# Mixer's output projection, first half: two-by-two blocks with seven products for eight

## The chip, the core and the metric

The kernel runs on one core of one Trainium2 chip. The time is that of one execution on the device, in microseconds (us). A core has engines that work side by side, each through its own queue in order: TensorE (PE, matrix products; PEld is its loading of weights), VectorE (DVE), ScalarE (ACT), GpSimd (POOL), and SyncE (SP), which issues DMA transfers; GpSimd issues some too. Matrix products are collected in PSUM banks, which ACT and DVE read; operands lie in SBUF.

## The reference: what is computed

One decoder layer for a prompt of 512 tokens and 64 sample tokens (576 columns in all), width 1024. The mixer runs 16 SSM heads and 4 mLSTM heads side by side, gates them, and projects both back to 1024:

```python
y_ssd = (y_ssd + d_skip[:, None] * xs).reshape(bsz, length, SSM_INNER) * jax.nn.silu(z)
y_ssd = _rms(y_ssd.reshape(bsz, length, SSM_GROUPS, SSM_INNER // SSM_GROUPS)).reshape(bsz, length, SSM_INNER) * g_ssm_out
...
h_ml = _rms(h_ml).reshape(bsz, length, ML_INNER) * g_mlstm_out * jax.nn.sigmoid(og)
mix = jnp.concatenate([y_ssd.astype(x.dtype), h_ml.astype(x.dtype)], axis=-1) @ w_out
x = x + _rms(mix) * g_post_mix
```

Cross-attention over a memory and a SwiGLU feed-forward layer follow. The first half of the output projection is `y_ssd` times rows 0 to 1023 of `w_out`, the second half `h_ml` times the other rows.

## The kernel before

**Products.** Activations lie transposed: 8 tiles of 128 channels, 576 columns of tokens. Every operand is split into a high part, rounded to the type that PE takes at full rate (`fp32r`), and a low part, the rest; ACT casts the high part, DVE (or GpSimd) subtracts to get the low one. A product is then three matmuls: high by high, high by low, low by high (L215, L216, L218 in `gemm`). Weights come tile by tile over SP's queue into `raw` (2 buffers), and become `whi` and `wlo` (3 buffers each) in `split_w`.

**Ahead of the change.** The last eight of the input projections (`in_tile(29 + j)`, output `ps_in`) make the output gate, each in two halves of 256 and 320 columns, 24 matmuls a half. `og_evac` takes each half: DVE multiplies it by the row factor into one of two `tmp` buffers (L1133), ACT takes the tanh (L1134), DVE multiplies it onto the mLSTM output in `qk` (L1136), and for the second half GpSimd copies the sample columns to `ogs` (L1138). `ps_in` has three PSUM banks. Between these halves the order places the last of the mLSTM heads: `ps_s`, `dm` (L966, L973), then for each of four chunks `ps_n` (L983, L985), its copy to `num` (L986), `ps_c` (L988) and the state's update (L993); then the head's norm (`head_norm`: ACT's sums of squares L938, small DVE steps L941 to L954, one GpSimd step L950), the scaling of `num` (L1000) and its transposition on PE (`ps_ht`, L1004). `gn_apply` normalises the SSM output in two groups of four tiles (`xs`, L1122) and splits it into `mixs_h` and `mixs_l`.

**The half that changes.** `out1(j)` makes one tile of 128 outputs from 8 tiles of `mixs`, in two halves of columns (256 and 320): 8 x 8 x 3 x 2 = 384 matmuls into `ps_o`, each half copied by ACT to `f_mix` (L1154). Beside it ACT and DVE make `mixm_h` and `mixm_l`, the operands of the second half, from `qk` (L1160, L1161), and `presplit` fetches weight tiles of later stages over GpSimd's queue (`prel`, L1251), splits them on ACT and DVE (L1244, L1245) and stores the low part for later (L1246). The second half, `out2`, adds its products to `f_mix` on DVE (L1288).

**What sets the order.** The program is written stage by stage; a scheduler that knows the tiles and their places in memory orders each engine's queue at build time. `tc.issue_after` holds a step back behind another one. Where a tile takes a place in memory that another one held, it waits for the last user of that place.

Of the kernel before, what the change touches and what calls it, by code (L numbers as in the profile page):

```python
# [11 lines left out]
F32 = mybir.dt.float32  # L12
# [7 lines left out]
P = 128  # L20
T = 576
# [94 lines left out]
def build(nc, tc, ctx, I, O):  # L116
# [324 lines left out]
    ghalf = ml.tile([P, KT], F32, name="ghalf")  # L441
    V.tensor_scalar(ghalf, PAR("g_ml"), 0.5, None, op0=ALU.mult)
# [668 lines left out]
    mixs_l = SL(2, "mixs_l", F32R)  # L1111
    gn_rc = {}
# [4 lines left out]
    def gn_apply(g):  # L1117
# [3 lines left out]
        for j in range(4 * g, 4 * g + 4):  # L1121
            V.scalar_tensor_tensor(y[:, j, :], y[:, j, :], PAR("g_ssm", j), rb, op0=ALU.mult, op1=ALU.mult)  # L1122
            split(mixs_h[:, j, :], mixs_l[:, j, :], y[:, j, :])
# [4 lines left out]
    ogs = zp.tile([P, KT, TS], F32, name="ogs")  # L1128
# [17 lines left out]

    f = SL(5, "f_mix")
    evs = []

    def out1(j):  # L1150

        with tc.issue_after(ht.ins) if j == 0 else ExitStack():
            gemm2([(*split_w(I["wout"][j, 0], cut=1024), KT)], act(mixs_h), act(mixs_l),
                  lambda t0, n, ps: evs.append(A.copy(f[:, j, t0:t0 + n], ps)), "ps_o1")  # L1154

    out1(0)
    for j in range(8):
        hm = qk[:, 4 * (j % 2) + j // 2, 0:TP]
        with tc.issue_after((evs[0] if j > 2 else htc).ins):
            A.activation(mixm_h[:, j, 0:TP], hm, AF.Copy, scale=ghalf[:, j:j + 1])  # L1160
        V.scalar_tensor_tensor(mixm_l[:, j, 0:TP], hm, ghalf[:, j:j + 1], mixm_h[:, j, 0:TP].bitcast(F32),  # L1161
                               op0=ALU.mult, op1=ALU.subtract)
    o4 = ogs.rearrange("p (h d) t -> p h d t", d=2)
    for d in range(2):
        V.scalar_tensor_tensor(o4[:, :, d], o4[:, :, d], 1.0, qk[:, 4 * d:4 * d + 4, TP:T], op0=ALU.add, op1=ALU.mult)
    V.tensor_tensor(ogs, ogs, ghalf.unsqueeze(2).to_broadcast([P, KT, TS]), op=ALU.mult)
    split(mixm_h[:, :, TP:T], mixm_l[:, :, TP:T], ogs)
    stv.close()


# [62 lines left out]
    PRE = [("xo", 0), ("xo", 1), ("g", 0), ("u", 0), ("g", 1), ("u", 1), ("g", 2), ("u", 2)]  # L1233
    pre = dr.tile([P, len(PRE), 1024], F32, name="pre")

    ahead = []

    def presplit(n, left=1):

        while len(ahead) > left:  # L1240
            n_, t_ = ahead.pop(0)
# [20 lines left out]
    for j in range(8):  # L1262
        if j:
            out1(j)
# [1212 lines left out]
```

## Time and profile before

| what | value |
|---|---|
| three runs | 1074.66, 1076.41, 1076.59 us (median 1076.41) |
| the profiled execution | 1074.69 us, its span 1072.9 us |
| granted TensorE clock | 0.999 |
| first half of the output projection | 384.0 to 433.8 us of the span |
| second half | 433.8 to 484.4 us |
| last gate halves, last mLSTM head | 342 to 384 us |

The times of the table's last rows are read from the first and last `ps_o` matmuls. The profile gives each engine's busy time, the chain of work that ended last, groups of instructions (count, busy time, mean of one), a timeline, and busy times by stretch of the span. A matmul's own duration (about 0.3 us) is longer than the distance between two starts, since matmuls are pipelined.

### The profile page before, as it was taken

The page shows a single profiled execution, that of the slowest core. Times are in us where ns is not written, and L with a number is a line of the kernel's source. Part 1 is how long each engine was busy: PE and PEld are TensorE (multiplying, and loading weights), DVE is VectorE, ACT ScalarE, POOL GpSimd, SP SyncE. Part 2 cuts the span into 40 slices and gives each one's busy share as a digit, 9 for nine tenths or more (in the row PEclk, how much of TensorE's full clock was granted, in tenths as well). Part 3 has the DMA queues.
Part 4 walks back from the last instruction along what each step waited for, and adds up shares of the span by engine and source line. Part 5 has one row for each costly group of instructions (what it writes and reads, how often), then busy time and mean ns, then how long its engine had stood idle before and what let it go on. Part 6 is the DMA issues. An engine that isn't in the chain of part 4 may idle for free.

```text
span 1072.9 us, 20686 instructions
## 1 busy us (share of the span) xinstructions
PE 1063.1 (99%) x8096; PEld 1011.0 (94%) x8096; DVE 757.7 (71%) x1523; ACT 608.9 (57%) x1102; POOL 231.0 (22%) x305
## 2 busy tenths in 40 slices
PE   9999999999999999999999999999999999999997
PEld 8999887778999999999999989999999999999997
DVE  6798775658878774758755556766467887787556
ACT  7778523345654555655555445645566566656654
POOL 0454543313213111000154201100011111111000
PEclk9999999999999999999999999999999999999999
DMA  6776544425655349642468775743476687578532
GB/s 209 176 162 132 158 134 172 147 89 168 196 150 152 106 143 330 235 170 98 158 213 288 265 256 176 254 124 98 133 179 137 160 188 178 114 191 188 144 119 89
DMA packets 58965, 181.74 MB, mean 169 GB/s; under 512 B 6604, under 2 KB 12108, under 8 KB 58356
## 3 DMA queue, kind: packets, MB, share of 16 engines
q1 hardware_dynamic: 42884, 138.22, 38.7%
q0 software_dynamic: 15408, 41.43, 19.7%
q8 instruction: 63, 1.03, 0.4%
q10 hardware_dynamic: 576, 0.79, 0.2%
q14 instruction: 34, 0.28, 0.1%
HBM read 159.75 MB, written 20.65 MB: 168 GB/s over the span
## 4 chain that ended last, share of the span: by engine, by line
PE 98%; DVE 0%; DMA 0%; POOL 0%; issue 0%; ACT 0%; SPq 0%; DVEq 0%
PE ps_in L215 7%; PE ps_in L218 7%; PE ps_in L216 7%; PE ps_v L882 5%; PE ps_g L1946 3%; PE ps_u L1946 3%; PE ps_g L1945 3%; PE ps_o L218 3%; PE ps_o L216 3%; PE ps_u L1947 3%; PE ps_g L1947 3%; PE ps_o L215 3%; PE ps_u L1945 3%; PE ps_dn L1945 2%; PE ps_dn L1947 2%; PE ps_dn L1946 2%
## 5 line engine op out<-in xcount | busy, mean ns | idle before, releaser
L215 PE MATMUL ps_in<-uh,whi 128*128 128x320 f32 (+1 forms) x544 | 162.6, 299 | 0.0
L218 PE MATMUL ps_in<-uh,wlo 128*128 128x320 f32 (+1 forms) x544 | 161.6, 298 | 0.0
L216 PE MATMUL ps_in<-ul,whi 128*128 128x320 f32 (+1 forms) x544 | 161.1, 296 | 0.0
L191 ACT CAST whi<-raw 128x1024 fp32r<-128x1024 f32 (+1 forms) x104 | 105.4, 1015 | 93.3 <-PE ps_in L216 21.5
L198 DVE TENSOR_TENSOR wlo<-raw,whi 128x1024 fp32r<-128x1024 f32 (+2 forms) x97 | 95.3, 983 | 63.7 <-ACT whi L191 63.0
L215 PEld LDWEIGHTS ps_in<-uh,whi 128*128 128x128 f32 x544 | 102.3, 188 | 1.9 <-issue 0.8
L218 PEld LDWEIGHTS ps_in<-uh,wlo 128*128 128x128 f32 x544 | 102.2, 188 | 1.9 <-issue 1.3
L216 PEld LDWEIGHTS ps_in<-ul,whi 128*128 128x128 f32 x544 | 102.4, 188 | 0.5
L196 POOL DMA_DIRECT2D wlo<-win x31 | 27.2, 877 | 80.2 <-ACT wlo L195 69.9
L1945 PE MATMUL ps_g<-b,whi 128*128 128x288 f32 x144 | 42.4, 295 | 0.0
L1946 PE MATMUL ps_g<-b,whi 128*128 128x288 f32 x144 | 42.3, 294 | 0.0
L1946 PE MATMUL ps_u<-b,whi 128*128 128x288 f32 x144 | 42.2, 294 | 0.0
L1945 PE MATMUL ps_u<-b,whi 128*128 128x288 f32 x144 | 42.2, 294 | 0.0
L1905 DVE TENSOR_TENSOR wlo<-sw,whi 128x1024 fp32r<-128x1024 f32 (+1 forms) x26 | 29.6, 1139 | 16.8 <-ACT whi L1904 16.8
L1918 ACT CAST whi<-rawx 128x1024 fp32r<-128x1024 f32 (+1 forms) x26 | 25.6, 986 | 26.2 <-PE ps_dn L1946 13.3
L1895 ACT CAST whi<-raw 128x1024 fp32r<-128x1024 f32 (+1 forms) x26 | 25.6, 985 | 22.8 <-PE ps_g L1946 11.8
L215 PE MATMUL ps_xo<-qh,whi 128*128 128x288 f32 x128 | 38.2, 301 | 0.0
L216 PE MATMUL ps_xo<-ql,whi 128*128 128x288 f32 x128 | 37.8, 297 | 0.0
L218 PE MATMUL ps_o<-mixm_h,wlo 128*128 128x256 f32 (+1 forms) x128 | 37.5, 293 | 0.0
L216 PE MATMUL ps_o<-mixm_l,whi 128*128 128x256 f32 (+1 forms) x128 | 37.5, 293 | 0.0
L218 PE MATMUL ps_xq<-u2h,wlo 128*128 128x320 f32 (+1 forms) x128 | 37.5, 294 | 0.0
L218 PE MATMUL ps_o<-mixs_h,wlo 128*128 128x320 f32 (+1 forms) x128 | 37.4, 293 | 0.0
(788 smaller groups left out, 3855.6 us busy)
## 6 DMA issues: line engine op xcount, KB each, us to landing
raw<-win SPq DMA_DIRECT2D x35, 512.0 KB, 4.4
raw<-wout SPq DMA_DIRECT2D x17, 512.0 KB, 4.2
raw<-wxq SPq DMA_DIRECT2D x13, 512.0 KB, 4.7
raw<-wgate SPq DMA_DIRECT2D x13, 512.0 KB, 3.3
raw<-wup SPq DMA_DIRECT2D x13, 512.0 KB, 4.7
wlo<-win POOLq DMA_DIRECT2D x24, 256.0 KB, 5.6
kva<-vc SPq DMA_DIRECT2D x11, 512.0 KB, 5.9
raw<-wv SPq DMA_DIRECT2D x10, 512.0 KB, 4.0
```

Of the source, the lines that this page charges most:

```text
L191: casts.append(A.copy(hi[:, :n], raw[:, :n]))
L196: accs.append(G.dma_start(lo[:, a:b], src[:, a:b], accum_op=ALU.add))
L198: e.tensor_tensor(lo[:, a:b], raw[:, a:b], hi[:, a:b].bitcast(F32), op=ALU.subtract)
L215: mm(ps, wh, ah, start=i == 0, stop=False)
L216: products.append(mm(ps, wh, al, start=False, stop=False))
L218: m = mm(ps, tiles[order[c]][1], xh(order[c], t0, n), start=False, stop=c == len(tiles) - 1)
L882: mm(ps, a, b, skip_group_check=True, **kw)
L1895: s.c1 = A.copy(s.h1[:, s.all], s.r1[:, s.all])
L1905: V.tensor_tensor(s.l2[:, s.all], sw[:, s.all], s.h2[:, s.all].bitcast(F32), op=ALU.subtract)
L1945: mm(ps, wh, b[0][k], start=start and k == 0, stop=False, skip_group_check=True)
L1946: mm(ps, wh, b[1][k], start=False, stop=False, skip_group_check=True)
L1947: m = mm(ps, wl, b[0][k], start=False, stop=k == nk - 1, skip_group_check=True)
```

## The change

The eight output tiles are taken in four pairs. A pair's weights are a two-by-two block matrix (two output tiles by the two halves of the contraction, tiles 0 to 3 and 4 to 7), and the activations are one too (the two halves of the contraction by columns 0 to 287 and 288 to 575). The four blocks of the result are put together from seven products of sums of blocks instead of eight products of blocks. A product is 4 tiles x 3 matmuls of 288 columns; a pair is 84, all four 336.

The sums of activations are made once, in place in the gated SSM output (`xs`; `y` in the code) by GpSimd: four, each 128x4x288, and each is split into `tmh` and `tml` by ACT and DVE. The sums of weights are made for each pair: four GpSimd operations of 128x512, into `swm`, `rawm` and `raw`. `h4` and `ls`, a high and a low part, take columns of `mixs_h` and `mixs_l` that are no longer used. A pair runs as `early` (products 1, 2), then the previous pair's `late` (products 6, 7), then `mid` (3, 4, 5). Some products accumulate onto a bank after ACT has copied it out; `put` copies a block the first time and adds the second time on DVE.

Around it: `ogs` moves to the new pool `mixsums`, the `mixm` parts go behind the casts of pairs 0 and 1, `presplit`'s subtraction goes from DVE to GpSimd and most of its turns to the second half, and the loads of the memory (`memT`) with them.

```diff
@@ gn_apply(g)
-            split(mixs_h[:, j, :], mixs_l[:, j, :], y[:, j, :])
+            c = slice(0, T if g else 288)
+            split(mixs_h[:, j, c], mixs_l[:, j, c], y[:, j, c])
+        for m, o, a, b in ([(2, M12, M22, M12), (1, M22, M22, M11), (3, M21, M21, M22)] if g else [(0, M11, M12, M11)]):
+            G.tensor_tensor(o, a, b, op=ALU.subtract)
+            split(tmh[m], tml[m], o)
...
-    ogs = zp.tile([P, KT, TS], F32, name="ogs")
+    ogs = wo.tile([P, KT, TS], F32, name="ogs")
...
+    def mixm_parts(js, p_):
+        for j in js:
+            hm = qk[:, 4 * (j % 2) + j // 2, 0:TP]
+            with tc.issue_after(p_.cast.ins):
+                A.activation(mixm_h[:, j, 0:TP], hm, AF.Copy, scale=ghalf[:, j:j + 1])
...
-    def out1(j):
-
-        with tc.issue_after(ht.ins) if j == 0 else ExitStack():
-            gemm2([(*split_w(I["wout"][j, 0], cut=1024), KT)], act(mixs_h), act(mixs_l),
-                  lambda t0, n, ps: evs.append(A.copy(f[:, j, t0:t0 + n], ps)), "ps_o1")
...
+    class Mixed:
...
+            s.r1 = wp.tile([P, 1024], F32, name="raw", tag="raw", bufs=2)
+            s.r2 = wv.tile([P, 1024], F32, name="rawm", tag="rawm", bufs=2)
...
+            G.tensor_tensor(sm[:, HB], s.r2[:, HA], s.r2[:, HB], op=ALU.add)
+            split(h1, l1, s.r1)
+            G.tensor_tensor(sm[:, HA], sm[:, HB], s.r1[:, HA], op=ALU.subtract)
+            G.tensor_tensor(s.r2[:, HA], s.r1[:, HA], s.r2[:, HA], op=ALU.subtract)
+            split(h2, l2, sm)
+            G.tensor_tensor(s.r1[:, HB], s.r1[:, HB], sm[:, HA], op=ALU.subtract)
+            A.copy(h3, s.r2)
...
+            s.cast = A.copy(h4, k4(s.r1[:, HB]))
...
+        def mul(s, ps, w, b, start=True):
+            fh, fl = s.w[w]
+            for k in range(4):
+                mm(ps, fh[:, k, :], b[0][k], start=start and k == 0, stop=False, skip_group_check=True)
+                mm(ps, fh[:, k, :], b[1][k], start=False, stop=False, skip_group_check=True)
+                m = mm(ps, fl[:, k, :], b[0][k], start=False, stop=k == 3, skip_group_check=True)
+            return m
+
+        def put(s, a, i, ps, first):
+            o = f[:, s.j + a, ES[i]]
+            if first:
+                evs.append(A.copy(o, ps))
+            else:
+                V.tensor_tensor(o, o, ps, op=ALU.add)
+
+        def early(s):
+            s.x, y_ = s.bank(), s.bank()
+            with tc.issue_after(ht.ins) if s.j == 0 else ExitStack():
+                s.mul(s.x, 0, m11)
+            s.put(0, 0, s.x, True)
+            s.mul(y_, 1, m21)
+            s.put(0, 0, y_, False)
+
+        def mid(s):
+            s.mul(s.x, 2, tm[1], False)
+            s.put(0, 1, s.x, True)
+            s.z = s.bank()
+            s.mul(s.z, 3, tm[0])
+            s.mul(s.x, 4, tm[2], False)
+            s.put(1, 1, s.x, True)
+            s.put(1, 1, s.z, False)
+
+        def late(s):
+            s.mul(s.x, 5, tm[3], False)
+            s.put(1, 0, s.x, True)
+            s.mul(s.z, 6, m22, False)
+            s.put(0, 1, s.z, False)
...
-            V.tensor_tensor(t_, t_, h_.bitcast(F32), op=ALU.subtract)
+            G.tensor_tensor(t_, t_, h_.bitcast(F32), op=ALU.subtract)
...
+    for j in (0, 2, 4, 6):
+        pair_ = Mixed(j)
+        pair_.early()
+        if before:
+            before.late()
+        pair_.mid()
+        before = pair_
+        presplit(*((1, 0) if j < 4 else (2, 1) if j == 4 else (0, 0)), wv, ("pr", "prl"))
+        if j < 4:
+            mixm_parts(range(2 * j, 2 * j + 4), pair_)
...
-    for j in range(8):
-        if j:
-            out1(j)
-        presplit(min(len(turns), 1 if j else 2))
-
-        if j > 3:
-            k2 = slice(2 * j - 8, 2 * j - 6)
...
+    presplit(2, 0, at, ("pr", "prl", "mv"))
+    for j in range(4):
+        k2 = slice(2 * j, 2 * j + 2)
...
```

**The order that comes of it.** On GpSimd, the queue around the copies to `ogs`, at the end of the gate halves. Before (L1138 the copies, L950 a step of an mLSTM head's norm: 128x4 for the prompt, 128x1 for the samples; the last 128x4 is the last head's):

```order
L1138 COPY ogs<-tmp 128x64
L950 TENSOR_TENSOR hn_y<-hn_v,c_78 128x1
L1138 COPY ogs<-tmp 128x64
L196 DMA wlo<-win 128x512
L1178 MEMSET ssqm 128x64
L1178 MEMSET ssqo 128x64
L1138 COPY ogs<-tmp 128x64
L196 DMA wlo<-win 128x512
L1138 COPY ogs<-tmp 128x64 x2
L950 TENSOR_TENSOR hn_y<-hn_v,c_78 128x4
L1138 COPY ogs<-tmp 128x64
```

And now (L1147 the copies, L1131 the sums of activations):

```order
L950 TENSOR_TENSOR hn_y<-hn_v,c_78 128x1
L1131 TENSOR_TENSOR xs<-xs 128x4x288
L950 TENSOR_TENSOR hn_y<-hn_v,c_78 128x4
L1147 COPY ogs<-tmp 128x64 x4
L196 DMA wlo<-win 128x512
L1147 COPY ogs<-tmp 128x64
L196 DMA wlo<-win 128x512
L1131 TENSOR_TENSOR xs<-xs 128x4x288 x2
L1147 COPY ogs<-tmp 128x64
L1131 TENSOR_TENSOR xs<-xs 128x4x288
L1147 COPY ogs<-tmp 128x64 x2
```

Seven of the eight copies stood ahead of the last head's L950 (two of them above the piece shown); now all eight stand behind it, and the first sum ahead of it.

On DVE, the evacuations of the gate halves (`tmp<-ps_in`, L1133 before, L1142 now) around the end of the last mLSTM head. Before, from the last copy of `num`:

```order
L986 COPY num<-ps_n 128x257
L1133 TENSOR_TENSOR tmp<-ps_in,rxb 128x256
L203 TENSOR_TENSOR mixs_l<-xs,mixs_h 128x576 x4
L1133 TENSOR_TENSOR tmp<-ps_in,rxb 128x320
L198 TENSOR_TENSOR wlo<-raw,whi 128x1024
L941 SCALAR_TENSOR_TENSOR hn_d<-num 128x4
L1136 SCALAR_TENSOR_TENSOR qk<-tmp,qk 128x256 x2
L942 TENSOR_TENSOR hn_d<-hn_d,expnm 128x4
L1133 TENSOR_TENSOR tmp<-ps_in,rxb 128x256
L198 TENSOR_TENSOR wlo<-raw,whi 128x1024
L1133 TENSOR_TENSOR tmp<-ps_in,rxb 128x320
```

And now, from the end of that head's norm:

```order
L952 SCALAR_TENSOR_TENSOR hn_a<-hn_a,hn_v 128x4
L953 SCALAR_TENSOR_TENSOR hn_a<-hn_a,hn_y 128x4
L954 TENSOR_TENSOR hn_a<-hn_a,hn_d 128x4
L1000 TENSOR_SCALAR num<-num,hn_a 128x256 x4
L1142 TENSOR_TENSOR tmp<-ps_in,rxb 128x256
L1142 TENSOR_TENSOR tmp<-ps_in,rxb 128x320
L203 TENSOR_TENSOR tml_4033<-xs,tmh_4029 128x1152
L1145 SCALAR_TENSOR_TENSOR qk<-tmp,qk 128x256 x2
L1142 TENSOR_TENSOR tmp<-ps_in,rxb 128x256
L1145 SCALAR_TENSOR_TENSOR qk<-tmp,qk 128x256
L1142 TENSOR_TENSOR tmp<-ps_in,rxb 128x320
```

Before, evacuations stand among and ahead of the head's steps (L941 opens its norm); now the row of them begins behind its scaling, L1000, and twelve of the sixteen stand there.

On PE, the products of the last head's last chunks and its transposition `ps_ht`. Before, the end of the gate halves and the start of the projection:

```order
L216 MATMUL ps_in<-ul,whi 128x320
L218 MATMUL ps_in<-uh,wlo 128x320
L1004 MATMUL ps_ht<-c_78,num 128x128 x8
L215 MATMUL ps_o_4651<-mixs_h,whi 128x256
L216 MATMUL ps_o_4651<-mixs_l,whi 128x256
L218 MATMUL ps_o_4651<-mixs_h,wlo 128x256
```

And now:

```order
L983 MATMUL ps_n<-vt_1795,dm 128x257
L1074 MATMUL ps_hts<-c_78,hns 128x128 x2
L988 MATMUL ps_c<-vt_1795,kw 128x257
L985 MATMUL ps_n<-cst__3104,qs 128x257
L1004 MATMUL ps_ht<-c_78,num 128x128 x8
L215 MATMUL ps_in<-uh,whi 128x320
L216 MATMUL ps_in<-ul,whi 128x320
L218 MATMUL ps_in<-uh,wlo 128x320
```

Before, the last head's `ps_ht` was the last thing ahead of the projection, with all gate halves in front of it; now nine gate halves stand behind it, and ahead of it from the head's first `ps_n` on there is none.

On ACT, the first two pairs: `f_mix<-ps_o` copies a product out, `swm`, `rawm` and `raw` are weights, `mixs_h<-raw` is `h4`.

```order
L1227 COPY f_mix<-ps_o 128x288
L202 CAST whi<-swm 128x1024
L1205 CAST whi<-rawm 128x1024
L202 CAST whi<-raw 128x1024
L1208 CAST mixs_h<-raw 128x4x128
L1160 ACTIVATE mixm_h<-qk,par 128x512 x4
L1227 COPY f_mix<-ps_o 128x288
L202 CAST whi<-swm 128x1024
L1208 CAST mixs_h<-raw 128x4x128
L1160 ACTIVATE mixm_h<-qk,par 128x512 x4
L1227 COPY f_mix<-ps_o 128x288 x2
```

Where a copy stood between single casts before, the second copy of the first pair now stands behind three casts of weights, `h4` and four `mixm_h`, and the third behind two casts and four more.

102 lines of the change are left out of this document (67 added, 35 removed).

## The prediction

> **What bounds the kernel now.** I read the page first: busy times, then the chain that ended last.
>
> ```profile
> PE 1063.1 (99%) x8096; PEld 1011.0 (94%) x8096; DVE 757.7 (71%) x1523; ACT 608.9 (57%) x1102; POOL 231.0 (22%) x305
> PE 98%; DVE 0%; DMA 0%; POOL 0%; issue 0%; ACT 0%; SPq 0%; DVEq 0%
> ```
>
> TensorE (PE) is the bound everywhere: a matmul less is time saved, and a microsecond in which PE has to wait is time lost. Next come the busy times of three stretches: the last input projections with the last mLSTM head, then the half that is changed, then the second half.
>
> ```profile
> core 0: us, PE busy (x) PEld busy (x) DVE busy (x) ACT busy (x) POOL busy (x), PEclk, DMA share, GB/s
> 342.00:384.00 42.00, 42.00 (x308) 40.31 (x307) 34.52 (x83) 21.94 (x45) 8.44 (x13) 1.00 0.40 111
> 384.00:433.80 49.80, 49.80 (x387) 49.80 (x387) 29.83 (x40) 29.38 (x52) 6.91 (x13) 1.00 0.76 260
> 433.80:484.40 50.60, 50.60 (x393) 50.58 (x393) 33.54 (x59) 31.64 (x53) 3.84 (x7) 1.00 0.55 197
> L215 PE MATMUL ps_o<-mixs_h,whi x128: 276/304/365, 384.1 to 433.5; 128*128 128x256 f32 x64, 128*128 128x320 f32 x64
> L218 PE MATMUL ps_o<-mixs_h,wlo x128: 276/294/310, 384.4 to 433.8; 128*128 128x256 f32 x64, 128*128 128x320 f32 x64
> ```
>
> PE has no gap in any of them, at full clock; GpSimd (POOL) does almost nothing. The changed half is 384 matmuls from 384.0 to 433.8, 49.8 us or 129.7 ns for one of 288 columns on average. So the change can gain there, and it can only lose where PE is made to wait.
>
> **The saving.** 336 products of 288 columns stand for 384: 48 fewer. 48 x 0.1297 = **6.2 us** less on PE. The feed-forward stage has products of this shape:
>
> ```profile
> 902.53 0.29 PE L1945 MATMUL ps_g<-b,whi 128*128 128x288 f32 x1
> 904.78 0.30 PE L1947 MATMUL ps_u<-b,wlo 128*128 128x288 f32 x1
> ```
>
> They start 17 products apart, 132.4 ns each; 336 of these are 44.5 us, a saving of 5.3, the low end. I take 6.2, since a product of 256 and one of 320 in this half average the lower price.
>
> **The wait that the order brings.** DVE's evacuation of an output-gate half needs one of two `tmp` buffers; it comes free when GpSimd has copied to `ogs`. These copies now stand on GpSimd behind the last mLSTM head's normaliser (L950) and behind the first sum (L1131). So DVE's evacuations stand behind that head's scaling (L1000), and on PE nine gate halves stand behind its `ps_ht`. Before, these halves covered the head's whole chain of small steps. Now PE has one half (24 products) ahead of it and nothing else. The rows for the chain, all of before (the last three are groups: count, then busy us and mean ns):
>
> ```profile
> 345.31 4.04 DVE L1122 SCALAR_TENSOR_TENSOR xs<-xs,par,ssqg 128x576 f32<-128x576 f32 x4
> 349.27 1.11 DVE L966 SCALAR_TENSOR_TENSOR dm<-ps_d,CT,c 128x128 f32<-128x128 f32 x4
> 351.08 0.69 DVE L973 TENSOR_TENSOR dm<-dm,ps_s 128x512 f32<-128x512 f32 x1
> 358.54 0.48 DVE L993 SCALAR_TENSOR_TENSOR cst__3097<-cst__3089,scalem,ps_c 128x257 f32<-128x257 f32 x1 [0.56 <-PE ps_c L988]
> 359.40 0.43 DVE L986 COPY num<-ps_n 128x257 f32<-128x257 f32 x1 [0.39 <-PE ps_n L985]
> 365.32 3.00 DVE L1122 SCALAR_TENSOR_TENSOR xs<-xs,par,ssqg 128x576 f32<-128x576 f32 x4 [0.18 <-ACT ssqg L289]
> 371.82 0.42 ACT L938 ACTIVATE hn_jk<-num 128x256 f32<-128x256 f32 x1
> 380.01 0.16 DVE L948 TENSOR_TENSOR hn_v<-hn_v,hn_ss 128x4 f32<-128x4 f32 x1
> 380.21 0.17 DVE L949 TENSOR_SCALAR hn_v<-hn_v 128x4 f32<-128x4 f32 x1
> 382.68 1.14 DVE L1000 TENSOR_SCALAR num<-num,hn_a 128x256 f32<-128x256 f32 x4
> L988 PE MATMUL ps_c<-vt,kw x8: 377/380/380, 354.9 to 365.6; 128*128 128x257 f32 x8
> L950 POOL TENSOR_TENSOR hn_y<-hn_v,c 128x4 f32<-128x4 f32 x4 | 4.7, 1184 | 7.3 <-DVE hn_v L949 6.2 <-DVE rg_r L276 1.1
> L686 POOL TENSOR_TENSOR hs<-hs,decp 128x512 f32<-128x512 f32 x6 | 6.3, 1042 | 15.7 <-DVE hs L687 11.1 <-DVE hs L684 4.6
> L198 POOL TENSOR_TENSOR wlo<-raw,whi 128x512 fp32r<-128x512 f32 x17 | 30.0, 1767 | 31.4 <-ACT whi L191 31.2
> ```
>
> Up to 345.3 the two kernels do the same. Then DVE: L966 1.11, four `xs` (3.00 or 4.04, by these two rows), L973 0.69: `dm` is ready at 350.1 to 351.2; I take 350.9. Four chunks follow one another, each a product (0.38), a copy (0.43), another product (0.38) and a state update (0.48), 1.67 us; with hand-offs I take 1.8: 358.1. ACT's sums of squares (0.42 and a reading): 359.1. Six small DVE steps at 0.2 (380.01 to 380.21 is one) with one low part of the gated SSM output between: 360.7. GpSimd is at the first sum by then, begun at 359.8 when the last low part is written: 1152 columns at 1042 ns for 512 are 2.35 us, at 1767 ns 4.0; so it ends at 362.2, and L950 (1.18) at 363.4. Four small steps, 0.8, and L1000, 1.14, to 365.2; `ps_ht` ends at 365.7. Nine halves follow, 5 of 320 and 4 of 256 columns, each of 24 products: at 129.7 ns for 288 columns 28.4 us, with 0.6 of small products 29.0. The first product of the projection starts at 394.7 and not at 384.1: **+10.6**, from 7.5 (chunks of 1.0) to 14 (slow `xs`, slow sum, 1.5 more in hand-offs).
>
> **The clock after the wait.** Between its last product of the fourth chunk and `ps_ht` PE has nothing for some 7.5 us. What the clock does then is shown at the end of the kernel, where the last matmul stops at 1065.9:
>
> ```profile
> 1065.00:1066.00 1.00, 0.88 (x6) 0.65 (x6) 0.51 (x3) 0.31 (x2) 0.00 (x0) 1.00 0.00 0
> 1069.00:1070.00 1.00, 0.00 (x0) 0.00 (x0) 0.41 (x1) 0.00 (x0) 0.00 (x0) 1.00 1.01 371
> 1070.00:1071.00 1.00, 0.00 (x0) 0.00 (x0) 0.00 (x0) 0.00 (x0) 0.00 (x0) 0.68 1.04 387
> 1071.00:1072.00 1.00, 0.00 (x0) 0.00 (x0) 0.00 (x0) 0.00 (x0) 0.00 (x0) 0.50 0.15 53
> ```
>
> It falls to half after 4.5 us of nothing (0.68 in that slice: at 1070.4). How soon it comes back no row shows; if that takes as long as the fall, 4.4 us at half speed lose **2.2 us**, from 0 (the wait is broken up) to 4.4 (it takes twice as long, or happens again at the second wait below). The Trainium skill ("TensorE: Matmul & The Clock Gate", Part 1) has the clock halved after an idle window of about 3.4 us and given back after as much sustained work. The fall agrees; by its 3.4 us the loss would be 1.7, and the sum half a microsecond less.
>
> **The first pair of tiles.** Its weight sums have to be made before its third product, and nothing is there to cover them (groups of both halves, 384 to 484):
>
> ```profile
> 395.85 1.16 POOL L1251 DMA_DIRECT2D prel<-wxo  x2 [7.53 <-DVE mixm_l L203]
> L191 ACT CAST whi<-raw 128x1024 fp32r<-128x1024 f32 x17 | 17.8, 1048 | 16.4 <-PE ps_o L216 13.3 <-PE ps_in L216 3.0
> L198 DVE TENSOR_TENSOR wlo<-raw,whi 128x1024 fp32r<-128x1024 f32 x17 | 20.8, 1224 | 15.7 <-ACT whi L191 15.7
> L1160 ACT ACTIVATE mixm_h<-qk,ghalf 128x512 fp32r<-128x512 f32 x8 | 5.1, 724 | 0.0
> L1154 ACT COPY f_mix<-ps_o 128x320 f32<-128x320 f32 x8 | 3.3, 416 | 0.0
> ```
>
> GpSimd's last `ogs` copy comes 1.8 us after the last gate half, at 396.5; two `prel` loads stand before the sums (1.16): 397.7. L1199 and L1201, 1.04 each, 399.8; ACT's cast 1.05, DVE's low part 1.22: 402.1. PE has two products, 24 matmuls, 3.1 us from 394.7, and stops at 397.8: **+4.3** (3.3 with a quicker last copy, 6 with sums at 1.77). Next, product five accumulates on the bank that ACT copies after product three. On ACT that copy stands behind three casts of weights, `h4` (about 0.6) and four `mixm_h` (0.72 each): from 400.9, 400.9 + 2.1 + 0.6 + 2.9 + 0.4 = 406.9, where PE asks at 402.1 + 2 x 1.57 = 405.3. That is 1.6 to 1.8, and the next copy stands behind the second pair's four `mixm_h` too, some 0.5 more: **+2.5** (0 to 4).
>
> After that a pair has 84 matmuls, 10.9 us on PE, against four sums on GpSimd (4.2 us at 1.04, 7.1 at 1.77), 5 to 8 us of ACT and as much of DVE. Here the products hide everything: if that cover goes, it is the third rival. The activation sums stand on GpSimd and their low parts on DVE among the last gate halves, ahead of the third product; that DVE keeps PE's pace there with these added is costed at nothing, and what it would cost otherwise is in the third rival.
>
> **The second half.** The memory's eight `memhl` with their squares, and six of eight `preh` casts, are now beside the second half, where ACT was busy 31.64 of 50.6 us; in its first units ACT has about 7.7 us for 6.25 on PE. Three buffers of weights and the banks take most of that: **+1** (0 to 3). The subtractions of `prel` go from DVE (1.2 us each) to GpSimd; off the path.
>
> **Sum.** -6.2 + 10.6 + 2.2 + 4.3 + 2.5 + 1 = +14.4. On the profiled execution's 1074.69 us that is 1089.1; the median of the runs is 1.7 higher than that execution, so about 1090 for a median. The low ends give +4.6 (1079.3; 1081 as a median), the high ends +26 (1101; 1102).
>
> **Rivals.**
> 1. *The chain is covered after all, and the saving arrives (faster).* It needs the last head to be done by the time PE has finished the one half ahead of `ps_ht`, and the first sums to be ready at the third product. That speaks for an idle GpSimd (8.44 us busy of 42). Against it: the chain's own steps take 15 us from `dm`, at durations that the trace shows, where it would have to take less than PE's own small products in it, about 5 us. The price: 1074.7 - 6.2 = 1068.5, 1070 as a median. 4 in 100 with the cases near it.
> 2. *Only the first pair waits, or the gate wait is half as long.* If the chain's small steps overlap more than I let them, say 5 us in place of 12.8 with the clock: 1074.7 - 6.2 + 5 + 4.3 + 1 = 1079, and with none of it 1074 to 1076. 12 in 100.
> 3. *GpSimd becomes the bound of the pairs.* The same subtraction takes 1042 ns alone and 1767 ns where DVE works on the other part of the same tile (the two GpSimd rows above). With all sums at 1767 ns, a `prel` subtraction of 2 to 3.6 us and its loads, a pair asks up to 11.8 us of GpSimd for 10.9 of PE: 1 us for each of the last two pairs, 2.3 more in the first, 1.6 in the chain, and 1 where DVE falls behind in the gate stage (four `xs` took 4.04 us once and 3.00 once): 1089 + 7 = 1096, 1098 as a median. 17 in 100. The Trainium skill ("GPSIMD Engine Reference", 8. Key points) says that GpSimd shares its SBUF interfaces with VectorE and that DVE instructions with two SBUF inputs contend; every low part here is one. The two rows agree; by it all sums beside low parts are at the slow price.
> 4. *The forecast*, 65 in 100. Over 1102, by something not on this list, 2.
>
> **How the numbers follow.** The likeliest case is the forecast: 1090. The range from 1077 to 1102 takes in the forecast's ends, the second rival's upper part and the third. About 0.2% (2 us) is what a measurement of this kernel tells from no change; so faster 4 in 100, within it 6 (the second rival's lower part), slower 90.
>
> **What would show it.** In the profile after: the first `ps_o` at about 395 and not 384; PE idle for 9 to 12 us between 350 and 366, with the last head's `num` or `hn_a` as what ended it, and the granted clock below 1.00 behind it; a gap of 4 to 5 us after the first 24 `ps_o` products, ended by `swm`'s cast or low part; 10.9 us for each of the last pairs with no gap. If `ps_o` starts at 384 to 388, the reading of the order is wrong; if pairs take over 11.5 us each, GpSimd or ACT is the bound there; if the second half takes over 54 us, what was moved into it is.

## The result, and the profile after

The changed kernel takes 1102.38 us (median of four runs, 1101.34 to 1103.87), the kernel before 1075.74 (four runs, 1074.66 to 1076.59): 1.0249 times as long, with a 95% interval of 1.0231 to 1.0267. The forecast of 1090 had the direction, but the loss is 27 us, not 14, and the time lies just above the upper end of the range, 1102.

The page of the changed kernel, its busy times and the chain that ended last:

```profile
PE 1067.0 (97%) x8048; PEld 1010.7 (92%) x8048; DVE 791.3 (72%) x1543; ACT 617.0 (56%) x1114; POOL 287.4 (26%) x333
PE 80%; DVE 7%; DMA 6%; POOL 2%; issue 2%; ACT 2%; SPq 0%; DVEq 0%; ACTq 0%; POOLq 0%
```

PE was 98% of that chain and is 80% now; a fifth of the chain runs over the other engines and transfers. That isn't PE's idle time, which is 32.6 us (span less busy time) after 9.8 before. PE has 48 matmuls fewer, DVE only 20 instructions more, but 34 us more of busy time. The stretches that answer to the three of before (last gate halves and last head; the changed half; the second half), in busy us of each engine with the granted clock behind them:

```profile
core 0: us, PE busy (x) PEld busy (x) DVE busy (x) ACT busy (x) POOL busy (x), PEclk, DMA share, GB/s
342.00:397.00 55.00, 44.74 (x311) 41.99 (x310) 45.89 (x88) 25.03 (x50) 21.56 (x17) 0.94 0.25 67
397.00:450.00 53.00, 44.73 (x300) 43.40 (x300) 41.41 (x47) 26.48 (x42) 29.64 (x22) 0.90 0.45 150
450.00:509.20 59.20, 56.37 (x431) 55.62 (x430) 44.04 (x68) 40.08 (x70) 25.84 (x24) 1.00 0.72 258
```

PE idles in all three, and its clock is below 1.00 in two. The waits of PE between 345 and 510 us, in total, how often, and the longest (one more, of 0.2 us, is left out):

```profile
PE ps_ht L1004 <- DVE num L1000: 7.5, 1, 7.5
PE ps_o L1219 <- ACT whi L202: 4.3, 1, 4.3
PE ps_o L1221 <- DVE wlo L203: 4.0, 3, 1.9
PE ps_in L215 <- DVE tmp L1142: 2.4, 1, 2.4
PE ps_ss L249 <- DVE ssqm L303: 2.0, 1, 2.0
PE ps_o L218 <- DVE wlo L198: 0.5, 1, 0.5
PE ps_o L215 <- DVE f_mix L1382: 0.3, 1, 0.3
```

All but one of these wait for DVE. The first two were forecast (the last head's chain; the first pair's weight sums, at 404.7). The others, 9.2 us together, were not. What holds DVE is seen where the timelines of GpSimd and DVE are read side by side; the columns are start, duration, engine, instruction:

```profile
357.33 2.61 POOL L1131 TENSOR_TENSOR xs<-xs 128x1152 f32<-128x1152 f32 x1 [5.57 <-DVE hn_d L942]
```

```profile
357.36 0.18 DVE L943 RECIPROCAL hn_d<-hn_d 128x4 f32<-128x4 f32 x1
357.57 2.38 DVE L947 TENSOR_TENSOR hn_v<-hn_d 128x4 f32<-128x4 f32 x1
360.06 0.16 DVE L948 TENSOR_TENSOR hn_v<-hn_v,hn_ss 128x4 f32<-128x4 f32 x1
```

A DVE operation on 4 columns, 0.16 us otherwise, started while GpSimd made the first sum of activations and ended when that sum ended, 359.95 against 359.94. The low parts of the weights show the same as means: group by group in the stretch from 384 us on, after, against 1224 ns for 128x1024 and 745 ns for 128x512 before. First the `mixm_l` of before, then the groups of after:

```profile
L1161 DVE SCALAR_TENSOR_TENSOR mixm_l<-qk,ghalf,mixm_h 128x512 fp32r<-128x512 f32 x8 | 5.5, 745 | 0.0
```

```profile
L198 DVE TENSOR_TENSOR wlo<-raw,whi 128x1024 fp32r<-128x1024 f32 x11 | 17.2, 1563 | 7.7 <-ACT whi L191 7.7
L1162 DVE SCALAR_TENSOR_TENSOR mixm_l<-qk,par,mixm_h 128x512 fp32r<-128x512 f32 x8 | 9.0, 1172 | 0.0
L203 DVE TENSOR_TENSOR wlo<-raw,whi 128x1024 fp32r<-128x1024 f32 x4 | 8.0, 2012 | 0.0
```

### The profile page after: what moved, and what is told of

Its sections match the earlier page's. It is cut to its first block, busy times and chain, and to the rows that moved or that the text cites. A ratio compares the mean times of both kernels' runs of the same rounds, so it can differ in the third digit from the quotient of the medians.

```text
span 1099.6 us, 20673 instructions
## 1 busy us (share of the span) xinstructions
PE 1067.0 (97%) x8048; PEld 1010.7 (92%) x8048; DVE 791.3 (72%) x1543; ACT 617.0 (56%) x1114; POOL 287.4 (26%) x333
## 4 chain that ended last, share of the span: by engine, by line
PE 80%; DVE 7%; DMA 6%; POOL 2%; issue 2%; ACT 2%; SPq 0%; DVEq 0%; ACTq 0%; POOLq 0%
PE ps_in L215 6%; PE ps_in L218 6%; PE ps_in L216 6%; PE ps_v L882 5%; PE ps_g L2041 3%; PE ps_u L2041 3%; PE ps_g L2040 3%; PE ps_u L2042 3%; PE ps_g L2042 3%; PE ps_u L2040 3%; PE ps_dn L2040 2%; PE ps_dn L2042 2%; PE ps_dn L2041 2%; PE ps_dn L215 2%; PE ps_dn L218 2%
## 5 line engine op out<-in xcount | busy, mean ns | idle before, releaser
L191 ACT CAST whi<-raw 128x1024 fp32r<-128x1024 f32 (+1 forms) x96 | 97.0, 1011 | 81.6 <-PE ps_in L216 17.4
L198 DVE TENSOR_TENSOR wlo<-raw,whi 128x512 fp32r<-128x512 f32 (+2 forms) x89 | 89.2, 1003 | 59.8 <-ACT whi L191 58.5
L2000 DVE TENSOR_TENSOR wlo<-sw,whi 128x1024 fp32r<-128x1024 f32 (+1 forms) x26 | 29.6, 1140 | 17.2 <-ACT whi L1999 11.8
L198 POOL TENSOR_TENSOR wlo<-raw,whi 128x512 fp32r<-128x512 f32 x17 | 30.0, 1768 | 33.0 <-ACT whi L191 32.9
L216 PE MATMUL ps_xq<-u2l,whi 128*128 128x320 f32 (+1 forms) x128 | 37.3, 294 | 0.9 <-DVE u2l L1319 0.9
L215 PE MATMUL ps_o<-mixm_h,whi 128*128 128x256 f32 (+1 forms) x128 | 37.6, 294 | 0.3 <-DVE f_mix L1382 0.3
L215 PE MATMUL ps_xq<-u2h,whi 128*128 128x320 f32 (+1 forms) x128 | 37.6, 295 | 0.0
```

What stands on the lines that cost most here:

```text
L191: casts.append(A.copy(hi[:, :n], raw[:, :n]))
L198: e.tensor_tensor(lo[:, a:b], raw[:, a:b], hi[:, a:b].bitcast(F32), op=ALU.subtract)
L215: mm(ps, wh, ah, start=i == 0, stop=False)
L216: products.append(mm(ps, wh, al, start=False, stop=False))
L2000: V.tensor_tensor(s.l2[:, s.all], sw[:, s.all], s.h2[:, s.all].bitcast(F32), op=ALU.subtract)
```

## The experiments

The theories that the runs were to tell apart: **A**, the place of `ogs` in memory made the order, and the order the wait in the gate stage; **B**, that stage is late whatever the order, by GpSimd's sums; **C**, a two-input GpSimd operation holds DVE until it is over; **D**, DVE lacks time because of its work itself; **E**, formed after the third run, the first pair waits because the parts of the activation sums have no place in memory until the last head is done.

### ogs in its old place

```diff
-    ogs = wo.tile([P, KT, TS], F32, name="ogs")
+    ogs_ = zp.tile([P, KT, TS], F32, name="ogs_")
...
-                G.tensor_copy(ogs[:, j, :], t[:, 256:320])
+                G.tensor_copy(ogs_[:, j, :], t[:, 256:320])
...
+    ogs = wo.tile([P, KT, TS], F32, name="ogs")
+    A.copy(ogs, ogs_)
     stv.close()
```

> The changed kernel, with the copies to ogs made into the place that they had before (the pool of the tmp buffers) and one ACT copy of 128x512 more from there into the new pool. On GpSimd seven of the eight copies then stand ahead of the last head's norm again, on PE all gate halves ahead of its ps_ht. Theory A (the place of ogs alone made the order, and the order the wait): the first ps_o starts at 384 to 387 and not at 397, no idle of PE between 350 and 366, the clock stays at 1.00 there, and the time falls by 10 to 13 us, to 1089 to 1092. Theory B (the gate stage is late because GpSimd's sums and DVE's work on them are too much for it, whatever the order): first ps_o at 393 or later, time 1098 or more.

Measured: 1097.51 us (1096.98 to 1099.93), 4.9 below the change. The first `ps_o` starts at 389.4, 7.7 earlier, and the idle of 7.5 us ahead of `ps_ht` is down to 0.4. So the place did make the order, and the order the wait. But most of it came back one step later (and the clock fell behind a wait for `tmp`: from 384 to 389 us it was granted at 0.67). PE's three largest waits in this run:

```profile
PE ps_o L1221 <- ACT whi L202: 9.3, 1, 9.3
PE ps_o L1223 <- DVE wlo L203: 4.7, 3, 2.6
PE ps_in L215 <- DVE tmp L1142: 2.6, 2, 1.8
```

The start of the first pair went from 4.3 to 9.3 us. What PE waits for there, the cast of the weight sum `swm`, starts at 401.42. The rows of ACT and of GpSimd that lead to it:

```profile
389.60 1.07 ACT L1005 COPY qk<-ps_ht 128x512 f32<-128x512 f32 x2 [5.70 <-PE ps_ht L1004]
390.56 4.32 ACT L202 CAST tmh<-xs 128x1152 fp32r<-128x1152 f32 x4
394.77 0.78 ACT L1143 ACTIVATE tmp<-tmp 128x256 f32<-128x256 f32 x2
401.42 1.05 ACT L202 CAST whi<-swm 128x1024 fp32r<-128x1024 f32 x1 [3.44 <-POOL swm L1203]
```

```profile
395.62 1.40 POOL L1147 COPY ogs__4039<-tmp 128x64 f32<-128x64 f32 x1 [8.03 <-ACT tmp L1143]
398.77 1.27 POOL L1201 TENSOR_TENSOR swm<-rawm 128x512 f32<-128x512 f32 x1
```

The high parts of the activation sums (`tmh`) stand on ACT behind the last head's `ps_ht`, all four together, 4.3 us. Behind them stands the last gate halves' tanh, behind that GpSimd's last copies to `ogs`, two loads, and only then the weight sums. So the splits are 4.3 of the 9.3 us, and the queues behind them are the rest; the copy of `ogs` that this experiment adds on ACT is among them. In the program's layout `tmh2` and `tmh3` lie over the last head's `num`, which `ps_ht` reads, so these two can't be written earlier. `tmh0` and `tmh1` lie over its `dm` and `kw` and older tiles; the last products that read `dm` and `kw` start at 362.8 and 365.5, so their place was free 24 us before, and it is the order on ACT that makes them wait. In the changed kernel the head came early and these splits were hidden behind nine gate halves; with the old order they are in the open. Neither A nor B holds by itself: A's mechanism, with a bill that moves.

### All of the change's two-input operations from GpSimd to DVE

Every `G.tensor_tensor` that the change brought becomes `V.tensor_tensor`, for instance

```diff
-            G.tensor_tensor(sm[:, HB], s.r2[:, HA], s.r2[:, HB], op=ALU.add)
+            V.tensor_tensor(sm[:, HB], s.r2[:, HA], s.r2[:, HB], op=ALU.add)
```

> The changed kernel, with every two-input operation that it brought to GpSimd (4 sums of activations, 16 of weights, 8 subtractions of prel) on DVE; the order of ogs stays as it is. Theory C (a two-input GpSimd operation keeps DVE from starting its own two-input operations until it is over, so DVE loses more than the work weighs): DVE has 26 us more work but 30 us less stretching, the waits for wlo inside the pairs (1.8 and 1.9 us) and the waits of the second half go; 7 to 10 us faster than the change, 1092 to 1096. Theory D (DVE is short of time in these stages because of the work itself): DVE's extra work lands on the path, same as the change or slower, 1101 to 1115.

Measured: 1087.76 us (1084.65 to 1089.18), 14.6 below the change, where C had asked for 7 to 10; ratio to before 1.0114 (1.0096 to 1.0132). So it is C and not D, which had said same or slower. DVE has 28 instructions more and less busy time, 785.0 us after 791.3:

```profile
PE 1064.2 (98%) x8048; PEld 1009.2 (93%) x8048; DVE 785.0 (72%) x1571; ACT 616.5 (57%) x1114; POOL 232.7 (21%) x305
```

PE's waits between 345 and 510 us, of which two of any size are left:

```profile
PE ps_ht L1004 <- DVE num L1000: 6.5, 1, 6.5
PE ps_o L1219 <- ACT whi L202: 3.0, 1, 3.0
```

Not all of the gain is DVE's time. The sums are also shorter on DVE (0.69 us for 128x512, where GpSimd's took 1.44 to 1.66 on average), and by that the first pair's wait goes from 4.3 to 3.0.

### Both edits

The two diffs above in one kernel.

> Both edits together: ogs in its old place, and no two-input operation of the change on GpSimd. Theories A and C: the gains add, 18 to 22 us below the change, 1080 to 1085, what is left being the start of the first pair (4 us and the clock behind it). A and D: 1089 to 1100, with PE waiting for DVE in the gate stage. If the saving of 6 us is to be seen at all, the steady pairs take 10.9 to 11.1 us each here.

Measured: 1086.78 us, spread over 1083.34 to 1091.12; ratio to before 1.0111 (1.0077 to 1.0144). The gains don't add: the first `ps_o` starts at 385.1 and the first pair waits 7.7 us, where the kernel with the operations on DVE alone waited 6.5 at `ps_ht` and 3.0 here. This is what theory E was made from. Here too the weight sums stand behind the same queue: the `tmh` casts (4.33 us from 386.25), the tanh, the copies of `ogs`, and they begin at 394.1.

### The sums apart

The same exchange of `G` for `V` in the four lines that sum weights (16 operations), in the one that subtracts for `prel` (8), and in the one that sums activations (4), each alone.

> The changed kernel, with the 16 sums of weights alone on DVE (0.68 us each there, by DVE's 128x512 subtractions). Theory C: the low parts of the pairs take 1.22 and 0.68 us and not 2.3 and 1.7, the waits of 1.8 and 1.9 us for wlo shrink to under 0.5 us, the half clock behind the second one goes, the first pair's third product comes 1 us sooner; 4 to 7 us faster than the change, 1095 to 1098. Theory D: DVE carries 11 us more in 50, and the pairs of tiles are no shorter: 1101 to 1106.

> The changed kernel, with the 8 subtractions of prel alone back on DVE (1.22 us each). Theory C: on GpSimd each (2.4 us) held one DVE operation for 2.0 to 2.2 us; the second half's waits (2.8 us) go, and one of the holds in the pairs; 3 to 5 us faster than the change, 1097 to 1099.5. With the 8 us of e4_wsums_dve and those of e10_asums_dve it should add up to the 14.6 us of e2_sums_dve. Theory D: no difference, 1101 to 1104.

> The changed kernel, with the 4 sums of activations alone on DVE (1.35 us each). Theory C: each held one DVE operation for 2.1 to 2.4 us in the gate stage (a norm step, a low part of the SSM output, a gate product); the wait of 2.4 us for DVE at 391 goes, the first ps_o starts at 394 to 395 and not 397, and the first weight sums 2 us sooner; 3 to 5 us faster than the change, 1097 to 1099.5. Theory D: DVE has 5.4 us more in a stage where it is busy all the time from 380 on: no faster, 1102 to 1106.

Measured: 1094.35 us (weights), 1096.60 (`prel`), 1095.76 (activations): 8.0, 5.8 and 6.6 below the change, each more than expected and each clear of the change's runs (the highest are 1097.37, 1098.49 and 1096.66, the change's lowest 1101.34). Together these medians are 20.4, where all three at once gave 14.6. The profiled executions do add up: their spans are 4.0, 5.1 and 4.8 us shorter than the change's, 13.9 together, and 14.3 with all three at once. The excess of the medians lies within runs that spread over 2.3 to 4.9 us, and isn't shown to be more than that. Predicted places can be read off: with the sums of activations on DVE the 2.4 us wait for `tmp` is gone and the first `ps_o` starts at 393.8; with those of weights all three waits for `wlo` are gone. With `prel` on DVE the second half has no wait left. One prediction failed: with the sums of weights on DVE the half clock was to go with the waits for `wlo`, but the clock fell behind other waits instead, and its mean is 0.985 (the change: 0.991).

### Useless GpSimd work in the kernel before

To see the hold without the change: 28 additions, or 28 copies, of 128x512 on GpSimd beside the first half (the additions ran from 394 to about 457 us), into a part of memory that nothing reads. The diff is that of the additions.

```diff
+        if j:
+            for _ in range(4):
+                with tc.issue_after(evs[-1].ins):
+                    G.tensor_tensor(junk, mixs_h[:, 0, 0:512].bitcast(F32), mixs_h[:, 1, 0:512].bitcast(F32), op=ALU.add)
```

> The kernel before, with 28 useless GpSimd additions of two 128x512 inputs (from mixs_h into a part of memraw's slot that nothing reads) spread over the first half of the projection. Theory C: each holds whichever two-input DVE operation starts beside it until it is over; low parts of 1.22 us appear at 2 us and more, DVE's busy time between 384 and 484 (63 us before) rises by 12 to 25 us; the time stays within 4 us of before, since DVE had slack there. Theory D: DVE's durations stay at 1.22 and 0.68 us, and GpSimd's are the longer ones.

> The same with 28 useless GpSimd copies of one 128x512 input. If it is the two inputs on GpSimd's side that hold DVE: DVE's durations stay as before (1.22 and 0.68 us). If any GpSimd operation does: DVE's busy time rises by up to the copies' own time, 28 times 0.5 to 1 us.

Measured: with additions 1081.79 us, 1.0049 times before (1.0031 to 1.0067); with copies 1075.27, 0.9997 (0.9987 to 1.0007). The groups of DVE from 384 to 490 us, with additions:

```profile
L198 DVE TENSOR_TENSOR wlo<-raw,whi 128x1024 fp32r<-128x1024 f32 x16 | 24.7, 1542 | 4.6 <-ACT whi L191 4.5
L1245 DVE TENSOR_TENSOR prel<-prel,preh 128x1024 f32<-128x1024 f32 x8 | 15.5, 1933 | 6.9 <-ACT preh L1244 6.7
```

and with copies:

```profile
L198 DVE TENSOR_TENSOR wlo<-raw,whi 128x1024 fp32r<-128x1024 f32 x16 | 20.9, 1304 | 14.7 <-ACT whi L191 14.7
L1245 DVE TENSOR_TENSOR prel<-prel,preh 128x1024 f32<-128x1024 f32 x8 | 11.2, 1396 | 6.2 <-ACT preh L1244 6.1
```

Before, the first group is at 1224 ns and the second this:

```profile
L1245 DVE TENSOR_TENSOR prel<-prel,preh 128x1024 f32<-128x1024 f32 x8 | 9.8, 1226 | 7.7 <-ACT preh L1244 7.6
```

DVE's busy time from 384 to 434 us goes from 29.83 to 44.02 with additions and 32.53 with copies. C is shown in a kernel without the change, and it cost 6 us, where I had expected at most 4: DVE fell so far behind that PE waited 3.6 us for the memory's sums (`ps_ss`) in the second half. Copies hold DVE too, so two inputs on GpSimd's side aren't needed for it: in that stretch 13 copies (10.5 us of GpSimd) cost DVE 2.7 us, 17 additions (28.2 us) cost it 14.2.

### Fewer pairs with seven products

As in "Both edits", with the first pair of tiles, or the first two, made in eight products as before, from activations that are split in full again; these need no sums, and stand in front.

```diff
+    def direct(j):
+        fh, fl = split_w(I["wout"][j, 0], cut=1024)
+        for i in (1, 0):
+            ps = (MP if i else GP)("ps_o")[:, :288]
...
+        if j < 2:
+            direct(j)
+            direct(j + 1)
+            presplit(1, 0, wv, ("pr", "prl"))
+            continue
         pair_ = Mixed(j)
```

> As e3_both (ogs in its old place, no two-input operation of the change on GpSimd), and the first pair of output tiles made in eight products, as before (96 matmuls of 288 columns a tile pair; 372 to 384 in all are then 348), from the unsummed activations, which are split in full again; mixm's parts stand beside the second and third pair. Theory E (the first pair waits because the parts of the activation sums have no place in memory until the last mLSTM head is done, so the wait went from the gate stage to the first pair; 12.4 us of products that need no sums cover it): first ps_o at 382 to 385, no gap of PE over 1.5 us up to the second half, saving 4.7 us in the half; 1071 to 1078. Theory D (DVE is short of time for low parts, sums and adds, wherever they start): the waits come back at the second pair or in the second half, 1080 to 1087.

> As e5_direct1, with the first two pairs made in eight products (360 matmuls), mixm's parts beside them as before. Theory E: nothing waits, saving 3.1 us in the half; 1072 to 1076. Theory D: DVE has about 14 us less to do in the half than in e3_both, so what is left of its waits is small, 1076 to 1081, and this is faster than e5_direct1.

Measured: 1080.13 us with one such pair (1.0052 of before, 1.0030 to 1.0074) and 1075.92 with two (1.0000, 0.9989 to 1.0011). E is right about the start: there is no wait at the first pair. (In both a wait of 1.4 us stays in the gate stage.) But with three pairs of seven products PE waits for DVE later on, a row of its timeline and one of its waits:

```profile
404.12 0.40 PE L1223 MATMUL ps_o<-tmh,wlo 128*128 128x288 f32 x1 [1.70 <-DVE wlo L203]
```

```profile
PE ps_o L1223 <- DVE mixs_l L1208: 3.2, 1, 3.2
```

Only the second of them is theory D. Ahead of the first wait DVE itself sat idle for 2.46 us, since an addition to `f_mix` stood next in its queue and waited for a product of PE; that is an order, not a lack of time. Ahead of the second, which ends at 422.1, DVE was busy without a break (its row of the timeline, then the busy times of the stretch between the two waits):

```profile
401.87 0.45 DVE L1231 TENSOR_TENSOR f_mix<-f_mix,ps_o 128x288 f32<-128x288 f32 x1 [2.46 <-PE ps_o L1223]
```

```profile
404.12:418.90 14.78, 14.78 (x110) 14.54 (x110) 14.78 (x24) 10.87 (x18) 1.07 (x2) 1.00 0.37 135
```

So E, as to where the wait is (its reason, the place in memory, is not tested here), and D both hold, one behind the other: once nothing holds DVE and the start is covered, a third pair of seven products asks more of DVE than it has in that stretch. With two such pairs PE's waits in the half are down to 0.5 us.

### Two tries to keep more of it

Both with the sums of activations behind the gate halves; the second with these low parts:

```diff
-            split(h1, l1, s.r1)
+            casts.append(A.copy(h1, s.r1))
+            V.tensor_tensor(l1[:, HA], s.r1[:, HA], h1[:, HA].bitcast(F32), op=ALU.subtract)
+            A.activation(l1[:, HB], h1[:, HB].bitcast(F32), AF.Copy, scale=-1.0)
+            accs.append(G.dma_start(l1[:, HB], I["wout"][j, 0][:, HB], accum_op=ALU.add))
```

> As e6_direct2 (first two pairs in eight products, ogs in its old place, no two-input operation on GpSimd), with the sums of activations behind the gate halves, where nothing waits for them. Theory E: the last waits (1.4 us at 380 in the gate stage, 0.5 us at 419) go; with products of 288 columns at 131.7 ns, as they run, 360 of them are 47.4 us for 49.8; 1.5 to 2.5 us faster than before, 1073 to 1074.5. Theory D: DVE's sums and low parts move onto the first Strassen pair, and it is 1075 to 1077.

> As e5_direct1 (only the first pair in eight products), with the sums of activations behind the gate halves, and with half of the low parts of the first pair's and of each later pair's first weights made by a DMA that adds the weights onto the negative high part, as the input projections do, so that DVE has 5 us less to do. Theory D (DVE's time is what the pairs lack): the waits of 1.7 and 3.2 us that e5_direct1 had for low parts shrink to under 1.5 in all, 348 products of 131.7 ns are 45.8 us for 49.8; 1072 to 1075. If they don't shrink, the waits are set by when the weights and their sums arrive, and it is 1077 to 1081.

Measured: 1076.60 us (1.0010 of before, 0.9999 to 1.0021) and 1086.72 (1.0103, 1.0089 to 1.0117). The first changes nothing: the wait of 1.4 us in the gate stage stays, so the sums of activations aren't what makes it, and what does is open. The second is slower than either theory said. It took DVE's work away (PE's waits for DVE's `wlo` are down to 0.5 us) and put a transfer in its place, which comes too late; its two largest waits:

```profile
PE ps_o L1228 <- DMA wlo<-wout: 4.8, 2, 4.1
PE ps_o L1226 <- ACT whi L202: 3.0, 1, 3.0
```

No version that was run beats the kernel before.

## Why the prediction was right in direction and too small

By its own terms, for the profiled executions (spans 1072.9 and 1099.6 us, 26.7 apart):

| term | predicted | measured |
|---|---|---|
| 48 matmuls fewer | -6.2 | -5.5 |
| last head's chain and nine gate halves | +10.6 | +13.0, with the clock there |
| the clock, once, after that wait | +2.2 | 1.4 there (in the 13.0), and 4.4 at two later places |
| first pair, weight sums | +4.3 | +4.3 |
| first pair, copies behind `mixm_h` | +2.5 | 0 as such; 4.0 of waits for low parts |
| second half | +1 | +2.8 |

The last column makes +23.0. The stretch behind the second half is 1.9 us longer than before, with 0.85 of it one wait of PE for DVE; 1.8 us aren't assigned. As for the forecast's own sums: 1089.1 and 1.7 more make 1090.8, and the high ends 1102.5, where it wrote 1090 and 1102.

**Right: the place and the mechanism of the first two waits.** The first `ps_o` starts at 397.1, where 394.7 and 2.2 for the clock had been forecast. The parts are not quite those: the chain was done sooner (`ps_ht` ends at 364.8, at half clock, not 365.7, since `dm` was ready at 349.6, not 350.9, the four chunks took 1.6 us each, not 1.8, and the first sum began at 357.3, not 359.8), and the nine halves took 32.6 us, not 29.0, with a wait of 2.4 for DVE that came from the sums' holds (it is gone with the sums of activations on DVE). PE's idle time ahead of `ps_ht` is one gap of 7.55 us, as the working had it; the 9 to 12 us that were named as a sign did not come.

The first pair's gap was forecast at 4.3 and is 4.28, and that close an agreement is luck. The sums began 3.9 us behind the first `ps_o`, not 3.0, and the two of them took 2.6 us, not 2.1; against that the forecast counted 1.22 for DVE's low part, which the product's first matmul does not need: it starts at 404.70, behind the cast, when the low part has only begun (404.68).

**The saving was mis-sized by its shape.** Products of 288 columns start 131.9 ns apart in the changed half's undisturbed stretch, where those of 256 and 320 average 129.5. That was the low end that the prediction gave and did not take.

**The failed step: what GpSimd's sums cost DVE.** The prediction wrote "Here the products hide everything", and that DVE keeps PE's pace in the gate stage "is costed at nothing". It had DVE's low parts at 1.22 us, and knew contention only as a price on GpSimd (1042 against 1767 ns), with 1 us for DVE in its third rival. What the runs show in its place are 9.2 us of waits of PE for DVE that no term had: 2.4 for `tmp`, 4.0 for `wlo`, 2.8 in the second half. In the sum part of this is covered by 2.5 us for copies behind `mixm_h`, which did not come. The rule of the Trainium skill that stood beside the third rival ("GPSIMD Engine Reference", 8. Key points) names DVE instructions with two SBUF inputs among those that contend; the traces agree, and I put it on GpSimd's account alone. The runs show the size: with all these operations on DVE the kernel is 14.6 us faster, though DVE then does 28 operations more. It is this, rather than the copies on ACT, that makes those waits: each is gone when the operations beside it are made on DVE. PE waited for no copy behind the four `mixm_h`; with DVE's holds gone such a wait is 0.2 us.

**The clock fell three times, not once.** The upper end of that term allowed a second fall. At half clock PE worked for 2.8, 5.3 and 3.4 us in the three spells that begin at 358.8, 403.2 and 427.1; half of that is lost, 1.4, 2.7 and 1.7 us. The second fall stands behind the gap of the first pair, which was forecast; the third behind a wait for a low part, which was not.

**The rivals.** The third, GpSimd as the bound, had the nearest number (1098) and part of the mechanism: the sums were slower than 1042 ns. But GpSimd was busy for 29.6 of the 53 us from 397 to 450, so it was not the bound; it cost time by what it kept DVE from. The first, nothing waits, did not come; the kernel with two pairs of seven products is as near as it was reached, and it equals the kernel before.

**The wait changes its place.** Either the last head comes early and PE waits for its chain, or it comes late and the first pair waits for the splits and the queues behind them. The two kernels with `ogs` in its old place show the exchange (7.5 and 4.3 us against 0.4 and 9.3; with the operations on DVE 6.5 and 3.0 against 1.0 and 7.7). That memory is behind it, since the sums' parts lie where the last head's tiles lie, is argued from the layout: it fits two of the four high parts, and no run puts the parts elsewhere. The one cover that was tried and worked is work that needs no sums, and that gives up the pairs that save.

## What to carry to other kernels

Before work goes to an idle GpSimd, look at what runs on DVE at that time. Here 28 operations cost DVE about 32 us of waiting when GpSimd made them, and about 26 when DVE made them itself (estimates: 16 x 0.69 + 8 x 1.22 + 4 x 1.35 us, and that with the 6.3 us by which DVE's busy time fell), so they were better left on it. A method that saves matmuls pays with sums and splits on other engines: set their time against what those engines have free per block of work (here 1.4 us of PE saved for each pair). When a wait is removed by an order, look for the place in memory that made the order, since the wait may only change its address.

## What the runs showed of the hardware that was not expected

**GpSimd and DVE.** A DVE operation with two inputs in SBUF that started during a two-input GpSimd operation waited until that was over, whatever its own size: 2.38 us for 128x4 (above). One with a single tensor input was held too, on 128x2 in the second half of the changed kernel, by its line's group:

```profile
L272 DVE TENSOR_SCALAR rmem_v<-rmem_s x1: 2373/2373/2373, 495.8 to 495.8; 128x2 f32<-128x2 f32 x1
```

The line's other seven take 0.15 to 0.17 us. An operation that reads PSUM and one tile of SBUF beside a sum was not held; from the timelines of GpSimd and DVE:

```profile
385.22 2.74 POOL L1131 TENSOR_TENSOR xs<-xs 128x1152 f32<-128x1152 f32 x1 [2.10 <-DVE mixs_l L203]
```

```profile
385.34 0.48 DVE L1142 TENSOR_TENSOR tmp<-ps_in,rxb 128x320 f32<-128x320 f32 x1
385.74 3.30 DVE L203 TENSOR_TENSOR wlo<-raw,whi 128x1024 fp32r<-128x1024 f32 x1
```

The evacuation took its usual 0.48 us inside the sum. The low part behind it, with two tiles of SBUF, took 3.30 in place of 1.22: it ended at 389.04, 1.08 us behind the sum's end at 387.96, about what it takes alone. The hold goes the other way as well. A sum of weights that came to GpSimd while a low part ran on DVE took 2.27 us, where 1.27 is its time alone; it ended 1.1 us behind the low part:

```profile
404.68 1.23 DVE L203 TENSOR_TENSOR wlo<-swm,whi 128x1024 fp32r<-128x1024 f32 x1 [3.70 <-ACT whi L202]
```

```profile
404.76 2.27 POOL L1204 TENSOR_TENSOR raw<-raw,swm 128x512 f32<-128x512 f32 x1
```

So in these rows whichever of the two started first was done first. Starts on GpSimd are rough, though: one low part that is shown 0.09 us behind the start of a sum, at 379.81, was not held, and the sum took 3.41 us.

**The clock.** It changes in steps of 3.41 us: the three spells at half clock are 6.83, 6.83 and 3.41 us long, and the second and third (403.22 and 427.11) begin 13 and 20 such steps behind the first (358.84). Windows of the changed kernel around the third, with the clock as the third number from the end:

```profile
426.00:427.00 1.00, 0.16 (x1) 0.16 (x2) 1.00 (x2) 0.00 (x0) 0.07 (x1) 1.00 0.32 70
427.00:428.00 1.00, 1.00 (x6) 1.00 (x7) 1.00 (x2) 0.00 (x0) 1.00 (x1) 0.55 0.93 360
430.00:431.00 1.00, 1.00 (x7) 1.00 (x7) 0.00 (x0) 0.00 (x0) 0.92 (x2) 0.74 0.00 0
431.00:432.00 1.00, 1.00 (x10) 1.00 (x9) 0.00 (x0) 0.00 (x0) 1.00 (x1) 1.00 0.00 0
```

PE had been idle for only 1.87 us (425.0 to 426.8), and then ran at half speed for 3.4 us. A gap of 1.78 us at 416.3 had no such effect. Counted back from the fall at 427.1 in steps of 3.41 us, the first gap fills 55% of one piece, and the second is divided over two, with 0.5 and 1.2 us in them. So a wait of 1.9 us cost 3.6. A rule of more than half a piece idle fits both, but not every gap of the case. The wait for `tmp` at 391.1 left PE just as idle within one piece, and the clock stayed at 1.00 behind it; the two pieces, in the columns of the windows above:

```profile
389.56:392.97 3.41, 1.55 (x14) 1.35 (x12) 3.41 (x2) 0.00 (x0) 3.27 (x1) 1.00 0.00 0
423.70:427.11 3.41, 1.54 (x12) 1.31 (x11) 3.41 (x7) 1.26 (x3) 0.18 (x1) 1.00 0.13 28
```

Over all runs of this case, from 12 to 1060 us, every full-clock piece with PE busy for less than 37% was followed by half clock, none with over 51% was, and of seven between 45% and 50% four were. What decides there is open. The Trainium skill ("TensorE: Matmul & The Clock Gate", Part 1) gives the window of 3.4 us, which agrees with the pieces, and asks for a window of idling before the clock is halved; here a gap of little more than half of that was enough, though not always.
